# Low parts of the full-width weight tiles formed by an accumulating transfer

## The chip, the cores and the metric

The kernel runs on one core of one Trainium2 chip. The metric is device time in microseconds (us): the median of several executions. A core has five engines that run side by side and wait for each other only where data passes between them: TensorE (PE, matrix products; PEld is its weight load), VectorE (DVE), ScalarE (ACT), GpSimd (POOL) and SyncE (SP, which issues most transfers). A transfer (DMA) moves data between the chip's memory and the on-chip SBUF, or inside SBUF.

## The reference, cut to what matters

One decoder layer over 1024 prompt tokens and 8 single-token sequences, 1032 columns in all, model width 1024, everything in float32:

```python
h = rms_norm(x, ln1); proj = h @ w_in             # q, k, v, xr, xg, g_att, g_lru
o_att = window_attention(q, k, v, ...) @ w_o_attn
o_lru = (rg_lru(causal_conv(xr)) * gelu(xg)) @ w_o_lru
x = x + (sigmoid(g_att) * o_att + sigmoid(g_lru) * o_lru) @ w_out
x = x + (silu(h2 @ w_gate) * (h2 @ w_up)) @ w_down
x = x + sigmoid(rms_norm(x, ln3) @ w_ple_gate) * (p @ w_ple)
```

The outputs are the new activations, the last window of keys and values, the recurrent state and the last rows before the convolution.

## The kernel before, in words

TensorE multiplies in a reduced float format (fp32r). To keep float32 accuracy every operand is split in a high part, rounded to that format, and a low part, the raw value minus the high part. A product is then three passes: high by high, high by low, low by high (`passes`, L334). One full product (`product`, L343) is 8 row blocks x 3 passes x 3 column thirds of 344, that is 72 matmuls; the third pass of its first row block is the first that reads the low part of the weights.

Weight tiles follow a written list, `plan` (L155): 4 q tiles, 16 gate tiles, 16 xr/xg tiles, 8 `oa` tiles, 8 `ol`, 8 `out`, the gate/up pairs of the feed-forward part (which have a splitting of their own, L244 to L269), 32 `down` tiles, 2 `pp` and 8 `pg`. The q, gate, xr/xg, ol, out, pp and pg tiles are 1024 wide, 62 in number; `oa` (512) and `down` (768 or 640) are narrower. `weights` (L327) is called as a product is written down: it loads the raw tile two places ahead in the list (`wload`, L198) and starts `wsplit` (L223) of the next tile. Raw, high and low tiles have three buffers each (tags wraw, whi, wlo). `split` (L180) forms the high part on POOL (L181) and the low part on DVE (L187); two ticks lie between them, and L187 is queued behind the last eviction of a product (`issue_after(st["mul"])`). The first tile of the list is formed in the startup with `ordered=True` (L183).

The text of the kernel gives each instruction its engine and a place in an order of generators (`at`, `spawn`, `tick`); from this the Tile framework's planner makes each engine's queue with costs and ready times of its own, and may move an instruction forward when it holds it to be ready. Edges by `keep` and `issue_after` bind it. On the chip each engine works through its queue strictly in order, and an instruction that waits holds up everything behind it.

Besides weight tiles, ACT takes results out of PSUM, forms high parts of activations (L357) and does all exponentials, tanh and the like; POOL multiplies the attention weights (L728) and parts of the recurrence, and issues the transfers that double the q and k rows (`halves`, L632, the issue in L638). Those 20 transfers are the only ones issued by POOL.

Of the kernel before, what the change touches and what calls it, by code (L numbers as in the profile page):

```python
# [13 lines left out]
AF = mybir.ActivationFunctionType  # L14
ALU = mybir.AluOpType
# [35 lines left out]
def body(ctx, tc, d):  # L51
    nc = tc.nc
    V, A, G, TE, DMA = nc.vector, nc.scalar, nc.gpsimd, nc.tensor, nc.sync.dma_start
# [38 lines left out]
    def f(t):  # L92
        return t.bitcast(F32)
# [86 lines left out]
    def split(raw, hi, lo, a, b, ordered=False):  # L180
        G.tensor_scalar(hi[:, a:b], raw[:, a:b], 1.0, 0.0, ALU.mult, ALU.add)  # L181
        if ordered:
            keep(V.tensor_tensor(lo[:, a:b], raw[:, a:b], f(hi[:, a:b]), ALU.subtract))  # L183
            return
        yield 2
        with tc.issue_after(st["mul"]):
            V.tensor_tensor(lo[:, a:b], raw[:, a:b], f(hi[:, a:b]), ALU.subtract)  # L187
# [35 lines left out]
    def wsplit(i, ordered=False):  # L223
        if i >= len(plan):
            return
        if paired(i):
            yield from pair_pre(i)
            return
        n = src(plan[i])[1]
        raw = raws.pop(i)  # L230
        hi, lo = whl(str(i))
        ready[i] = (hi, lo)
        yield from split(raw, hi, lo, 0, n, ordered)
# [676 lines left out]
    def recur(c, ps):  # L910
# [17 lines left out]
        wh = wp.tile([P, 256], F32R, tag="axh", name=f"axh{c}", bufs=1)  # L928
        wl = wp.tile([P, 256], F32R, tag="axl", name=f"axl{c}", bufs=1)
        yield from split(wr, wh, wl, 0, 256)  # L930
        xch = hi_of(f"xc{c}", xc)
        yield REC[3]
# [477 lines left out]
```

## Time and profile before

| | |
|---|---|
| time, median of 3 runs (lowest, highest) | 1600.42 us (1599.16, 1601.59) |
| the profiled execution's own time | 1602.14 us |
| its span, first to last instruction | 1600.4 us |
| TensorE busy | 1573.8 us (98%) |
| VectorE, ScalarE, GpSimd busy | 899.9, 527.9, 412.4 us |
| granted TensorE clock, mean | 0.995 |

Busy is the time in which an engine executes; an engine that stands at 98% leaves 26.6 us of the span without a matmul. In the lists of groups each line gives the busy total, the mean of one instruction in ns, and the idle time of that engine just before such instructions with what ended it. In a timeline the columns are start, duration, engine, line, operation, tile written and tiles read, shape, and in brackets the idle time before.

### The profile page before, as it was taken

Reading aid. Unit: us, or ns where it says so; the run is one execution under the profiler, and the core shown is the slowest. Engines: PE = TensorE matmul, PEld = TensorE weight load, DVE = VectorE, ACT = ScalarE, POOL = GpSimd, SP = SyncE. Lnnn points to the kernel's source line nnn. Section 1 sums busy time; section 2 is a strip of 40 time slices with the busy share of each in tenths; the row PEclk is TensorE's granted clock in tenths of the full one; section 3 lists DMA queues with packets and bytes.
Section 4 is the critical chain, followed back from the end, with each engine's and each line's share of the span. In section 5 each row is a group of like instructions: output and inputs, shape, how many; then the busy total and the mean of one; then the engine's idle time right before and its main releaser. Section 6 shows DMA issues by size and latency. Waiting matters only on the chain.

```text
span 1600.4 us, 25144 instructions
## 1 busy us (share of the span) xinstructions
PE 1573.8 (98%) x10763; PEld 1549.6 (97%) x10763; DVE 899.9 (56%) x1047; ACT 527.9 (33%) x785; POOL 412.4 (26%) x291
## 2 busy tenths in 40 slices
PE   8999999999999999999989999999998999999998
PEld 7999999999999999999989999999998999999998
DVE  8668555645778684355765555555555432436534
ACT  5652332314646651132633333333333110103201
POOL 4342211212232231012144444444442110011100
PEclk9899999999999999999999999999999999999999
DMA  5364122221111342333122222222225421312121
GB/s 191 79 166 125 54 103 83 83 73 35 55 43 34 109 159 81 106 123 129 53 80 80 80 80 80 80 80 79 78 75 215 167 93 57 116 55 88 30 90 53
DMA packets 46733, 145.78 MB, mean 91 GB/s; under 512 B 6645, under 2 KB 11038, under 8 KB 46622
## 3 DMA queue, kind: packets, MB, share of 16 engines
q1 hardware_dynamic: 44786, 138.80, 25.7%
q0 software_dynamic: 1600, 5.29, 1.6%
q8 instruction: 84, 1.38, 0.3%
q14 instruction: 27, 0.22, 0.0%
q10 hardware_dynamic: 236, 0.10, 0.0%
HBM read 107.45 MB, written 31.44 MB: 87 GB/s over the span
## 4 chain that ended last, share of the span: by engine, by line
PE 90%; DVE 3%; issue 2%; ACT 2%; DMA 1%; POOL 1%; SPq 0%; DVEq 0%; POOLq 0%; ACTq 0%
PE psd L338 15%; PE psgt L338 10%; PE psol L338 6%; PE psout L338 6%; PE psxr L338 6%; PE pspg L338 5%; PE psxg L338 5%; PE psq L338 2%; PE pspp L338 1%; PE o L751 1%; PE psrx L943 1%; PE psoa L1018 1%; PE pt L736 1%; PE psu10x L320 1%; PE psg6x L320 1%
## 5 line engine op out<-in xcount | busy, mean ns | idle before, releaser
L181 POOL TENSOR_SCALAR wh<-wr 128x1024 fp32r<-128x1024 f32 (+3 forms) x102 | 104.8, 1028 | 629.5 <-PE psd L338 222.8
L187 DVE TENSOR_TENSOR wl<-wr,wh 128x1024 fp32r<-128x1024 f32 (+3 forms) x101 | 118.8, 1178 | 10.9 <-POOL wh L181 10.9
L1075 DVE TENSOR_TENSOR x<-psd,x 128x1032 f32<-128x1032 f32 x32 | 39.4, 1232 | 128.8 <-PE psd L338 128.8
L1204 POOL TENSOR_TENSOR g<-g,n2r 128x1032 f32<-128x1032 f32 x22 | 54.2, 2466 | 142.5 <-DVE wl L242 126.1
L249 POOL TENSOR_TENSOR wsA<-wr 128x512 f32<-128x512 f32 x22 | 38.6, 1756 | 131.9 <-DVE wl L242 126.6
L253 DVE TENSOR_TENSOR wl<-wr,wh 128x1024 fp32r<-128x1024 f32 x22 | 26.9, 1225 | 67.3 <-ACT wh L250 67.3
L722 ACT ACTIVATE s<-s,st 128x256 f32<-128x256 f32 (+1 forms) x64 | 31.1, 489 | 77.8 <-DVE st L717 76.5
L728 POOL TENSOR_TENSOR s<-s,st 128x1024 f32<-128x1024 f32 (+1 forms) x16 | 28.6, 1787 | 98.1 <-DVE st L727 87.9
L240 ACT ACTIVATE wh<-wsA 128x1024 fp32r<-128x1024 f32 x22 | 23.3, 1060 | 91.5 <-issue 80.7
L242 DVE TENSOR_TENSOR wl<-wsB,wh 128x1024 fp32r<-128x1024 f32 x22 | 39.7, 1805 | 4.5 <-ACT wh L240 4.5
L252 POOL TENSOR_TENSOR wsA<-wsA,wr 128x512 f32<-128x512 f32 x22 | 38.7, 1757 | 1.6
L250 ACT ACTIVATE wh<-wr 128x1024 fp32r<-128x1024 f32 x22 | 23.3, 1060 | 47.2 <-PE psout L338 5.7
L1294 ACT ACTIVATE pg<-pg 128x1032 f32<-128x1032 f32 (+3 forms) x10 | 9.0, 895 | 88.3 <-DVE pg L96 79.9
L1217 DVE TENSOR_TENSOR u<-u,g 128x516 f32<-128x516 f32 x33 | 34.9, 1058 | 3.8 <-POOL g L1204 2.4
L96 DVE TENSOR_TENSOR pg<-pspg,n3r 128x1032 f32<-128x1032 f32 x7 | 8.6, 1232 | 48.9 <-PE pspg L338 48.9
L262 POOL TENSOR_TENSOR wsB<-wr,wr 128x512 f32<-128x512 f32 x22 | 33.8, 1538 | 7.9 <-DVE wl L242 7.9
L96 DVE TENSOR_TENSOR xr<-psxr,r1r 128x1032 f32<-128x1032 f32 x8 | 9.9, 1233 | 44.9 <-PE psxr L338 44.9
L1043 DVE SCALAR_TENSOR_TENSOR gl<-gl,psol 128x1032 f32<-128x1032 f32 x8 | 9.8, 1229 | 43.3 <-PE psol L338 43.3
L263 POOL TENSOR_TENSOR wsB<-wr,wsA 128x512 f32<-128x512 f32 x22 | 34.1, 1551 | 0.1
L925 DVE SCALAR_TENSOR_TENSOR xc<-xr,sm,xc 128x1021 f32<-128x1021 f32 (+2 forms) x24 | 30.7, 1277 | 5.9 <-ACT xc L919 5.9
L709 DVE TENSOR_TENSOR s<-s,bias 128x512 f32<-128x512 f32 (+1 forms) x32 | 19.7, 653 | 24.1 <-PE s L705 23.8
L970 POOL TENSOR_TENSOR hg<-h,xg 128x1032 f32<-128x1032 f32 x8 | 25.5, 3186 | 26.3 <-DVE h L966 22.7
(1691 smaller groups left out, 5065.1 us busy)
## 6 DMA issues: line engine op xcount, KB each, us to landing
wr<-w_in SPq DMA_DIRECT2D x36, 512.0 KB, 3.6
ad<-u SPq DMA_DIRECT2D x22, 516.0 KB, 2.6
a<-ad SPq DMA_DIRECT2D x22, 516.0 KB, 5.3
wr<-w_gate SPq DMA_DIRECT2D x22, 512.0 KB, 3.6
wr<-w_up SPq DMA_DIRECT2D x22, 512.0 KB, 3.6
sg<-gt SPq DMA_DIRECT2D x16, 516.0 KB, 2.8
gl<-sg SPq DMA_DIRECT2D x16, 516.0 KB, 4.5
wr<-w_down SPq DMA_DIRECT2D x16, 384.0 KB, 3.1
```

The lines of the kernel that those rows point to most:

```text
L181: G.tensor_scalar(hi[:, a:b], raw[:, a:b], 1.0, 0.0, ALU.mult, ALU.add)
L187: V.tensor_tensor(lo[:, a:b], raw[:, a:b], f(hi[:, a:b]), ALU.subtract)
L242: V.tensor_tensor(hl[1][:, :n], raw, f(hl[0][:, :n]), ALU.subtract)
L249: G.tensor_tensor(s[:, n:2 * n], b[:, :n], b[:, n:2 * n], ALU.add)
L252: G.tensor_tensor(s[:, :n], s[:, n:2 * n], a[:, :n], ALU.subtract)
L262: G.tensor_tensor(s[:, :n], a[:, :n], b[:, :n], ALU.subtract)
L263: G.tensor_tensor(s[:, n:2 * n], a[:, n:2 * n], e["s21"][:, :n], ALU.subtract)
L320: TE.matmul(ps[:, c, :QC], ww[:, w], xx[:, c * QC:(c + 1) * QC], start=first and kk == 0 and n == 0, stop=True if not last else kk == nk - ...
L338: TE.matmul(ps[:, c, :CH], ww[:, w], xx[:, c * CH:(c + 1) * CH], start=first and n == 0, stop=last and n == 2)
L1075: V.tensor_tensor(v3(t), ps[:, :, :CH], v3(t), ALU.add)
L1204: G.tensor_tensor(t, t, r, ALU.mult)
L1217: V.tensor_tensor(o, o, g, ALU.mult)
```

## The change

In `split`, a full-width tile (b == 1024) that is not the ordered one no longer has its low part formed by DVE. ACT writes minus the high part into the low tile, and a transfer issued from POOL's queue adds the raw tile onto it in SBUF. The two ticks and the edge behind the last eviction are gone for these tiles, 61 in number. The ordered tile and the narrower tiles stay as they were.

```diff
         G.tensor_scalar(hi[:, a:b], raw[:, a:b], 1.0, 0.0, ALU.mult, ALU.add)
         if ordered:
             keep(V.tensor_tensor(lo[:, a:b], raw[:, a:b], f(hi[:, a:b]), ALU.subtract))
+            return
+        if b == 1024:
+            A.activation(lo[:, a:b], f(hi[:, a:b]), AF.Copy, scale=-1.0)
+            G.dma_start(f(lo[:, a:b]), raw[:, a:b], accum_op=ALU.add)
             return
         yield 2
         with tc.issue_after(st["mul"]):
```

## Rows read from the trace of the kernel before

**Rows 1.** The page, part 1: busy us of each engine, share, instructions

```profile
PE 1573.8 (98%) x10763; PEld 1549.6 (97%) x10763; DVE 899.9 (56%) x1047; ACT 527.9 (33%) x785; POOL 412.4 (26%) x291
```

**Rows 2.** What PE waited for: total us, times, longest

```profile
PE r1ps L384 <- ACT r1sh L357: 2.7, 1, 2.7
...
PE r1ps L385 <- DVE r1sl L365: 1.7, 1, 1.7
...
PE psoa L1018 <- DVE wl L187: 0.4, 1, 0.4
```

**Rows 3.** Groups by form: busy us, mean ns, idle before and releasers

```profile
L187 DVE TENSOR_TENSOR wl<-wr,wh 128x1024 fp32r<-128x1024 f32 x61 | 82.8, 1358 | 6.4 <-POOL wh L181 6.4
L181 POOL TENSOR_SCALAR wh<-wr 128x1024 fp32r<-128x1024 f32 x62 | 72.6, 1171 | 383.7 <-PE psol L338 81.5 <-PE pspg L338 51.5 <-PE psxr L338 43.6
...
L250 ACT ACTIVATE wh<-wr 128x1024 fp32r<-128x1024 f32 x22 | 23.3, 1060 | 47.2 <-PE psout L338 5.7 <-PE psu2y L320 2.1 <-PE psu5y L320 2.1
```

**Rows 4.** Timeline of the startup, DVE, ACT and PE

```profile
36.81 2.35 DVE L187 TENSOR_TENSOR wl<-wr,wh 128x1024 fp32r<-128x1024 f32 x2
39.08 1.22 DVE L365 TENSOR_TENSOR r1sl<-x,r1sh 128x1032 fp32r<-128x1032 f32 x1
...
36.93 1.06 ACT L357 ACTIVATE r1sh<-x 128x1032 fp32r<-128x1032 f32 x1 [6.20 <-DVE x L569]
...
40.36 0.65 PE L385 MATMUL r1ps<-r1sl,ones_r 128*128 128x344 f32 x1 [1.66 <-DVE r1sl L365]
```

**Rows 5.** Timeline in the ol stage, POOL, SP's queue and PE

```profile
624.90 1.05 POOL L181 TENSOR_SCALAR wh<-wr 128x1024 fp32r<-128x1024 f32 x1 [10.30 <-PE psol L338]
...
627.72 0.33 SPq L212 DMA_DIRECT2D wr<-w_out  x1
...
647.60 1.05 POOL L181 TENSOR_SCALAR wh<-wr 128x1024 fp32r<-128x1024 f32 x1 [10.30 <-PE psol L338]
...
648.76 0.48 PE L338 MATMUL psol<-hg0h,wl 128*128 128x344 f32 x2
```

**Rows 6.** Timeline around the first ol product, POOL, ACT and PE

```profile
579.60 1.04 POOL L181 TENSOR_SCALAR wh<-wr 128x1024 fp32r<-128x1024 f32 x1 [4.60 <-DMA wr<-w_ol]
...
580.71 1.05 ACT L357 ACTIVATE hg3h<-hg 128x1032 fp32r<-128x1032 f32 x1
...
592.04 0.63 PE L338 MATMUL psol<-hg0h,wl 128*128 128x344 f32 x3
```

**Rows 7.** POOL's own transfers, L638: ns min/median/max of the issue; landing in us

```profile
L638 POOL DMA_DIRECT2D kd<-kh x4: 522/533/725, 70.6 to 72.4; - x4
...
DMA to landing us min/median/max: 2.9/4.4/7.7
```

**Rows 8.** Transfers issued by SP: count, KB each, median us to landing

```profile
wr<-w_in SPq DMA_DIRECT2D x36, 512.0 KB, 3.6
...
wr<-w_oa SPq DMA_DIRECT2D x8, 256.0 KB, 2.7
```

**Rows 9.** Stage 135 to 341 us: busy us (instructions) of PE, PEld, DVE, ACT, POOL

```profile
135.00:341.00 206.00, 205.33 (x1285) 193.08 (x1284) 115.49 (x251) 61.32 (x202) 41.29 (x30) 1.00 0.23 79
```

**Rows 10.** Timeline of one attention unit, DVE, POOL and PE

```profile
161.25 1.29 DVE L742 TENSOR_TENSOR p<-pt,p 128x512 fp32r<-128x512 f32 x2 [1.58 <-ACT p L738]
...
163.35 1.90 POOL L728 TENSOR_TENSOR s<-s,st 128x1024 f32<-128x1024 f32 x1 [10.20 <-DVE st L727]
...
163.62 0.39 PE L751 MATMUL o<-p,vth 128*128 128x512 f32 x1
...
172.62 1.03 PE L736 MATMUL pt<-ident,s 128*128 128x128 f32 x8
```

**Rows 11.** Startup windows: busy us as in rows 9, then granted clock, DMA share, GB/s

```profile
35.00:41.00 6.00, 1.66 (x6) 1.01 (x5) 5.20 (x5) 1.98 (x2) 0.00 (x0) 0.75 0.31 79
41.00:45.00 4.00, 4.00 (x17) 4.00 (x16) 0.00 (x0) 2.94 (x7) 0.01 (x1) 0.52 0.36 143
...
55.00:59.00 4.00, 4.00 (x18) 3.93 (x17) 2.12 (x3) 2.53 (x4) 1.36 (x1) 0.57 0.43 131
```

## The prediction

> **What bounds the kernel now.** I read the page's first part, then what PE waited for, then the timelines around the weight tiles. PE is busy 1573.8 us of a span of 1600.4 us [rows 1], so 26.6 us are all that a better hidden splitting could give back, and PE's list of waits says how little of that belongs to the low parts [rows 2]: the only PE wait that names a low part of weights is 0.4 us, at a narrow tile that the change leaves alone. One more is indirect. At 36.81 us DVE forms two low parts in 2.35 us, and the low part of the first norm's sum (r1sl) starts behind them at 39.08, though its input r1sh was ready at 37.99 (36.93 + 1.06) [rows 4]; PE waits 1.66 us for r1sl. The reader is to see in the rest that weights are formed far ahead. POOL writes a high part at 624.90, the moment a product ends and gives its buffer back; two products later the same happens at 647.60 (11.35 us each), and only in the product that starts then is the tile of 624.90 read, in its low part at 648.76 [rows 5]: 23.9 us of lead.
>
> **The change part by part.** The sum is made against the profiled execution, 1602.14 us (span 1600.4 and 1.74 around it); the median shown is 1600.42, 1.72 below, and I carry the difference over to it.
>
> *Removed from DVE:* 61 subtractions, 82.8 us in all, 1.36 us each [rows 3]. DVE is busy 899.9 us, off the bound, so 59 of them are worth nothing to PE. The two at 36.81 are worth the delay of r1sl: 39.08 - 37.99 = 1.09 us. What is late next is r1sh itself, which PE already waits for (2.7 us), and it does not depend on them. The gain is at least nothing (if the planner puts other DVE work in the place) and at most 1.66 us, the whole wait. I take -1.1.
>
> *Added on ACT:* 61 copies with factor -1, same shape and kind as the copy of 1.06 us [rows 3]: 65 us on an engine busy 527.9. They wait for POOL's high part (1.17 us on average), and behind them in ACT's queue stand the evictions and exponentials. In the startup the cover is ACT's idle gap of 6.20 us before r1sh [rows 4]. In the attention stage, where 13 tiles are formed, ACT is busy 61.3 of 206 us, 30% [rows 9]; if the moments are unrelated, 4 of 13 copies meet work and push it back by up to 1.06 us. The shortest cover there is between DVE's low part of the probabilities, done at 162.54, and the matmul that uses them at 163.62: 1.08 us [rows 10]. 1.06 fits in 1.08, barely. Below nothing is excluded, since ACT only gets more work. I take 0; without cover it is 4 x 1.06 = 4.2 us, and it is the second rival that says when.
>
> *Added on POOL:* 61 issues. The trace has 20, of half as many partitions, at 0.52 to 0.73 us [rows 7]. Twice the rows, and a second read for the addition, give at most 4 x 0.52 = 2.1 us; I take 1.0, twice the short one. Before it POOL waits for ACT's copy, 1.06 us when ACT is free. Behind it stand other high parts, which have the lead above, and in the attention stage the multiplication L728: it ends at 165.25 and PE transposes its result at 172.62 [rows 10], 7.4 us of cover against about 2. Cost 0.
>
> *The transfer itself* does not occur in the trace. Nearest rows: POOL's own SBUF transfers of 258 KB land in 2.9 to 7.7 us, median 4.4 [rows 7]; loads of 512 KB take 3.6 and of 256 KB 2.7 [rows 8], so 256 KB more cost 0.9. From 4.4: +0.9 for 512 KB, +1.8 for reading the destination as well, 7.1 us. Lower end 2.9; upper end, all doubled twice, 4 x 7.7 = 30.8. From the start of the high part the low part is then ready after 1.05 + 1.06 + 1.0 + 7.1 = 10.2 us, against a lead of 23.9 in the ol stage. The shortest lead of a full-width tile is at the first ol product, which follows the half-length oa products: high part at 579.60, first use at 592.04 [rows 6], 12.4 us. 2.2 us are left there, and ACT stands in a close row of copies (580.71 is one of them) that can eat them: 0, at most a few us, see the first rival. The raw buffer comes free when the transfer has landed instead of when DVE is done (SP's next load went out at 627.72, 2.8 us after the high part began [rows 5]); 7.4 us later costs nothing while a buffer is needed again only three products, 34 us, after. The DMA engines are busy 23% in the attention stage [rows 9]; a load that shares them with the new transfer lands later by at most its 7.1 us, inside the same 34.
>
> The DMA page of the Trainium skill (DMA: Bandwidth & Descriptors, section Anatomy of one DMA — SWDGE (gpsimd) path) gives such transfers about 2.0 us plus bytes over 436 GB/s, an estimate of 3.2 us for 512 KB. The 258 KB would be 2.6 us by it, where this trace has a median of 4.4, so I go by the trace; by the page's figure the sum is the same and the tight tile has 6 us to spare.
>
> *Narrow tiles, the feed-forward pairs and the ordered tile:* unchanged, 0.
>
> *Sum:* -1.1 + 0 + 0 + 0 = -1.1 us: 1601.0 for an execution like the profiled one, 1599.3 for the median.
>
> **The rivals.**
>
> *The transfer is late (slower).* Everything but the landing takes 3.1 us, so the tight tile waits from a landing of 9.3 us on. For: the longest landing of the small ones is 7.7 us, and the second read is unknown. At twice 7.7, 15.4 us, that product starts 15.4 + 3.1 - 12.4 = 6.1 us late, and the time is 1599.3 + 6.1 = 1605.4. From 20.8 us on every ol product waits too; at 30.8 the three-product loop of 34 us grows by 10, 3.3 us a product, 200 us over 61 tiles, about 1800. Against that end: the longest landing in the trace is a quarter of it.
>
> The SBUF page of the skill (SBUF — State Buffer, section Who interferes with whom) says that GpSimd writes the descriptors of such a transfer and is shut out while VectorE runs a two-port instruction. It would add the length of that instruction to a landing. Here the issues beside busy DVE took 0.73 us at most, against 0.52 [rows 7], so I give it no chance of its own.
>
> *The queue heads (slower; the rival on the other side).* Place: ACT's queue in the attention stage. The planner may put the copy ahead of work that is ready while POOL is not: then ACT stands for the high part (1.17 us [rows 3]) and the copy (1.06), 2.23 against the 1.08 of cover [rows 10], 1.15 us of PE each time. It decides when more than 4 of the 13 tiles do it. For: the edge that kept the low part behind the evictions is gone, and ACT has no pin for the copy. Against: ACT is idle 70% of that stage [rows 9], and PE waits for no line of it now [rows 2]. 4 tiles: +4.6, 1603.9; all 13: +15, 1614; I take 7, +8.1, 1607.
>
> *The clock (faster).* After PE's idle stretch the granted clock is 0.75 and then 0.52 for 4 us, the lower of its two levels (1.2 of 2.4 GHz), and again 0.57 at 55 to 59 [rows 11]. A gap that is 1.1 us shorter may not bring it down: 4 x 0.48 = 1.9 us, 3.0 in all, 1597.4; with the second dip (4 x 0.43 = 1.7) 4.7, 1595.7. Against: the wait of 2.7 us for r1sh stays, and so most of the gap.
>
> That the change does not do what it says is no rival: the condition can only be met by those 61 tiles.
>
> **How the numbers follow.** About 0.2%, 3.2 us, is what a measurement of this kernel can tell from no change. Forecast 0.56 (its own range 1597 to 1602: 0.47 within 0.2%, 0.05 below, 0.04 above); queue heads 0.18 (0.15 slower, 0.03 within); late transfer 0.11 (0.09 slower, 0.02 within); clock 0.12 (0.10 faster, 0.02 within); another order of the planner, either way, 0.03 (0.02 faster, 0.01 slower). Faster 0.17, same 0.54, slower 0.29. The range reaches down past the clock's 1595.7 to 1594, and up past 1607 to 1611; it leaves out the end of the late transfer and the case of all 13 tiles.
>
> **What would show it.** Right: DVE's full-width group L187 gone; r1sl at about 38.0 in the startup; landing of the new transfers 5 to 9 us; no PE wait that names wl of more than 1 us; PE's busy time as before. The late transfer: a PE wait on the transfer of the low part at the first psol product. Queue heads: ACT's copies with idle time before them that ends with POOL's wh, and PE waits in L751 or L736. The clock: windows 41 to 45 and 55 to 59 near 1.0. The prediction is wrong if PE's waits outside the first 60 us grow by more than 3 us.

## The result and the profile after

The changed kernel takes 1613.49 us (median of 4 runs, 1612.45 to 1614.40) against 1601.01 for the kernel before, run beside it: a ratio of 1.0080 [1.0067, 1.0092], about 12.5 us slower. The prediction was 1599.3, with a range of 1594 to 1611. The profiled execution took 1612.45 us, its span 1610.7, so 10.3 us are to be found between the two traces (executions of one kernel lie up to 3 us apart). From here on line numbers are those of the changed kernel, 4 higher after L183.

The page of after, part 1, answers [rows 1]:

```profile
PE 1578.0 (98%) x10763; PEld 1552.8 (96%) x10763; DVE 822.4 (51%) x986; ACT 588.7 (37%) x846; POOL 464.7 (29%) x352
```

The work moved as forecast: DVE lost 77.5 us, ACT gained 60.8. PE is busy for 4.2 us more with the same number of matmuls, so some of them ran at a lower clock. The rest is in its waits (total, times, longest), to be read beside [rows 2]:

```profile
PE s L707 <- DVE dsb L794: 5.8, 1, 5.8
PE psgt L342 <- issue: 3.0, 1, 3.0
PE vt L617 <- ACT wl L186: 2.9, 1, 2.9
...
PE r1ps L388 <- ACT r1sh L361: 1.0, 1, 1.0
PE s L707 <- DVE oA0l L767: 0.9, 1, 0.9
```

Two waits are new, the first two, and neither names a weight tile. The third, in the startup, does name ACT's copy, but it stands for the 2.4 us that PE waited there for DVE's vraw before: here vraw ends at 51.80 us and the copy at 51.82. The start of each stage's first matmul says where they count:

```
us from the span's start    before    after    after - before
gates and attention          92.8      91.9     -0.9
xr/xg                       341.2     352.4    +11.2
oa                          542.4     553.5    +11.1
gate/up pairs               772.4     783.5    +11.1
down                       1225.5    1237.4    +11.9
pp                         1480.9    1490.5     +9.6
end of the last matmul     1595.7    1606.0    +10.3
```

The gate and attention stage alone loses 12.1 us; all that follows it together gains 0.9.

**The first wait, at 105 us.** The timeline of ACT and POOL in after (start, duration; in brackets the idle time before and who ended it):

```profile
102.62 0.47 ACT L498 ACTIVATE sbias<-bias 128x384 f32<-128x384 f32 x1
...
104.92 1.24 POOL L181 TENSOR_SCALAR wh<-wr 128x1024 fp32r<-128x1024 f32 x1 [6.59 <-PE psgt L342]
...
106.19 1.06 ACT L186 ACTIVATE wl<-wh 128x1024 fp32r<-128x1024 f32 x1 [3.10 <-POOL wh L181]
107.16 1.01 ACT L680 ACTIVATE q3raw<-psq 128x1032 f32<-128x1032 f32 x1
```

and that of PE:

```profile
104.65 0.63 PE L342 MATMUL psgt<-x7h,wl 128*128 128x344 f32 x3
108.27 0.72 PE L342 MATMUL psgt<-x0h,wh 128*128 128x344 f32 x3 [2.98 <-issue]
```

The planner put the copy of tile 7 (the fourth gate tile) ahead of q3raw, the eviction of the last q product. The copy waits for POOL's high part, that for a free high buffer, and the buffer comes free only when PE ends its product at 104.9. So the eviction stands behind work that waits for PE, and PE's next product waits for the accumulator that the eviction empties. (The profile names no releaser for this wait; PE starts 0.1 us after the eviction ends, at 108.17.) In the kernel before, ACT evicts at once:

```profile
103.58 0.47 ACT L494 ACTIVATE sbias<-bias 128x384 f32<-128x384 f32 x1
103.95 1.02 ACT L676 ACTIVATE q3raw<-psq 128x1032 f32<-128x1032 f32 x1
```

**The second wait, at 250 us.** DVE in after:

```profile
254.42 1.23 DVE L96 TENSOR_TENSOR gt<-psgt,r1r 128x1032 f32<-128x1032 f32 x1 [6.06 <-DMA sg<-gt]
255.57 0.27 DVE L794 TENSOR_TENSOR dsb<-ds,sbias 64x128 f32<-64x128 f32 x1
```

An eviction of a gate product needs a row buffer, and the row comes free when an earlier gate tile has been stored (sg<-gt). Behind it in DVE's queue stands dsb, which empties the accumulator that PE wants for the next scores. Before, the same instruction came without a wait:

```profile
246.59 1.23 DVE L96 TENSOR_TENSOR gt<-psgt,r1r 128x1032 f32<-128x1032 f32 x1
```

SP's queue in after (the decode step's cache loads KT and VS, its stores o_ks and o_vs, the gate's store):

```profile
223.60 0.34 SPq L216 DMA_DIRECT2D wr<-w_in  x1
224.06 0.67 SPq L197 DMA_DIRECT2D KT<-kc  x1
224.83 0.44 SPq L197 DMA_DIRECT2D VS<-vc  x1
225.32 13.11 SPq L775 DMA_DIRECT2D VS<-vdr  x1
238.54 0.37 SPq L777 DMA_DIRECT2D o_ks<-KT  x1
239.00 0.66 SPq L842 DMA_DIRECT2D sg<-gt  x1
251.87 0.34 SPq L778 DMA_DIRECT2D o_vs<-VS  x1
```

and before:

```profile
217.56 0.33 SPq L212 DMA_DIRECT2D wr<-w_in  x1
218.01 0.67 SPq L193 DMA_DIRECT2D KT<-kc  x1
219.27 0.26 SPq L193 DMA_DIRECT2D VS<-vc  x1
219.59 2.96 SPq L771 DMA_DIRECT2D VS<-vdr  x1
227.09 2.43 SPq L773 DMA_DIRECT2D o_ks<-KT  x1
230.39 0.38 SPq L838 DMA_DIRECT2D sg<-gt  x1
242.87 0.34 SPq L774 DMA_DIRECT2D o_vs<-VS  x1
```

The landings of the 16 stores sg<-gt, that is the time that the profile gives from issue to arrival, in before and in after:

```profile
DMA to landing us min/median/max: 2.6/2.8/15.0
DMA to landing us min/median/max: 2.6/2.6/15.3
```

The longest in each is the store here: from 230.39 to 245.4 in the kernel before, 1.2 us ahead of its need at 246.59, and from 239.0 to 254.3 in after. What is in its way is the load VS<-vc of 127 rows. In a stretch of before in which little else is on the way, the window's last columns (granted clock, DMA share, GB/s) are:

```profile
236.00:240.00 4.00, 4.00 (x29) 3.98 (x28) 2.56 (x8) 1.61 (x6) 0.00 (x0) 1.00 0.06 27
```

A share of 0.06 is one of 16 DMA engines. The page DMA: Bandwidth & Descriptors of the Trainium skill (section Why a DMA increments its semaphore by 16 and not by 1) says that a transfer uses the largest number of engines up to 16 that divides the slowest dimension of both its sides; 127 is prime, so one, and the 0.06 agrees. From its issue to that of o_vs, which waits for it and for the single row VS<-vdr behind it, 23.6 us pass in before and 27.0 in after. In after SP also stands 13.1 us in the issue of VS<-vdr (3.0 before), so the store is issued 8.6 us later. That isn't what decides: the store lands 2.5 us after the issue of o_vs in before and 2.4 in after, and 2.4 to 2.6 after it in the six other kernels below that keep the load whole and whose traces list this store's landing, where it was issued 12 to 16 us ahead of o_vs. It lands when the load is through.

**The clock after it** (windows; granted clock is the third number from the end):

```profile
250.00:256.00 6.00, 0.23 (x3) 0.10 (x1) 1.54 (x3) 0.00 (x0) 0.88 (x1) 0.78 0.79 186
256.00:262.00 6.00, 6.00 (x20) 5.10 (x21) 3.89 (x13) 1.19 (x5) 0.00 (x0) 0.50 0.78 269
262.00:270.00 8.00, 8.00 (x46) 7.38 (x46) 1.63 (x4) 3.17 (x11) 1.90 (x1) 0.90 0.01 2
```

When PE resumes after 5.8 us of standing, 6 us run at 0.50, the lower level (1.2 of 2.4 GHz), and the next 8 at 0.90: 3.0 + 0.8 = 3.8 us. The sum for the stage: 2.98 - 0.65 at 105 us (there was a gap of 0.65 at 111 before), 5.8 at 250, 0.7 more in small gaps at 135 and 143 us, and 3.8 of clock give 12.6 against 12.1.

### The profile page after: what moved, and what is told of

The parts are those of the page before. It is cut to its first block, busy times and chain, and to the rows that moved or that the text cites. A ratio compares the mean times of both kernels' runs of the same rounds, so it can differ in the third digit from the quotient of the medians.

```text
span 1610.7 us, 25263 instructions
## 1 busy us (share of the span) xinstructions
PE 1578.0 (98%) x10763; PEld 1552.8 (96%) x10763; DVE 822.4 (51%) x986; ACT 588.7 (37%) x846; POOL 464.7 (29%) x352
## 3 DMA queue, kind: packets, MB, share of 16 engines
q0 software_dynamic: 10384, 37.27, 12.1%
## 5 line engine op out<-in xcount | busy, mean ns | idle before, releaser
L186 ACT ACTIVATE wl<-wh 128x1024 fp32r<-128x1024 f32 x61 | 64.5, 1059 | 226.5 <-POOL wh L181 226.4
L187 POOL DMA_DIRECT2D wl<-wr x61 | 54.1, 892 | 89.7 <-ACT wl L186 74.2
L191 DVE TENSOR_TENSOR wl<-wr,wh 128x768 fp32r<-128x768 f32 (+2 forms) x40 | 36.0, 903 | 4.5 <-POOL wh L181 4.5
```

The lines of the kernel that those rows point to most:

```text
L186: A.activation(lo[:, a:b], f(hi[:, a:b]), AF.Copy, scale=-1.0)
L187: G.dma_start(f(lo[:, a:b]), raw[:, a:b], accum_op=ALU.add)
```

## The experiments

Theory after the traces: the loss has two places, ACT's queue at 105 us (the copy) and SP's at 250 us. The rivals for the second: SP's order, which the planner changed; the transfers themselves, by landing late or by sharing the DMA engines; the cache load. All ratios are against the kernel before on the same chip.

**1. Only the first 20 tiles; only the last 42.**

```diff
-        if b == 1024:
+        if b == 1024 and i < 20:        # the other kernel: i >= 20
```

> Only the 19 tiles of q, gate and attention (plan index below 20) take the low part by copy and transfer; the other 42 are formed by DVE as before. Theory (the loss is made in the gate and attention stage alone): 1612 to 1615, PE idle about 3 us near 105 us and about 6 us near 250 us as in the changed kernel. Rival (the loss needs all 61 tiles, by load on the DMA engines or by the clock over the whole span): 1600 to 1606.

> Only the 42 tiles from plan index 20 on (recurrent inputs, ol, out, pp, pg) take the new path; q, gate and attention tiles as before. Theory: 1598.5 to 1601.5, no PE wait over 1 us that names a weight tile after 341 us. Rival (all 61 share the loss): 1606 to 1610.

Measured: 1612.18, 1.0073 [1.0058, 1.0088], gaps of 2.98 us at 105 and 5.48 at 251; and 1601.96, 1.0010 [1.0000, 1.0020], 0.5 us above the range of its theory. The 19 tiles of the q and gate products make the loss; the other 42 cost 0.1%, 0.2% at most.

**2. The two halves of the change apart.** First DVE forms minus the high part and the transfer stays; then ACT copies as in the change and DVE adds.

```diff
-            A.activation(lo[:, a:b], f(hi[:, a:b]), AF.Copy, scale=-1.0)
+            yield 2
+            with tc.issue_after(st["mul"]):
+                V.tensor_scalar(lo[:, a:b], f(hi[:, a:b]), -1.0, None, ALU.mult)
```
```diff
-            G.dma_start(f(lo[:, a:b]), raw[:, a:b], accum_op=ALU.add)
+            yield 2
+            with tc.issue_after(st["mul"]):
+                V.tensor_tensor(lo[:, a:b], raw[:, a:b], f(lo[:, a:b]), ALU.add)
```

> All 61 tiles; minus the high part is formed by DVE, behind the evictions as the subtraction was, instead of by ACT, and the transfer adds the raw tile as in the change. SyncE's order in the gate stage is then that of the kernel before. Theory (one half of the loss is ACT's queue head near 105 us, the other half a spill store that SyncE issues late because its order changed): both gone, 1599 to 1603. Rival (the transfer itself, its DMA load or its late release of the raw buffer): the wait near 250 us and most of the loss stay, 1607 to 1613.

> All 61 tiles; ACT copies minus the high part as in the change, and DVE adds the raw tile, behind the evictions, instead of the transfer. SyncE's order in the gate stage is that of the kernel before. Theory: if ACT stands with the copy ahead of the last q eviction near 105 us also here, PE idles 3 us there and 1603 to 1606 comes out; the wait near 250 us is gone. Rival (ACT alone makes the whole loss): 1610 to 1614. Second rival (ACT costs nothing, all is the transfer): 1598 to 1601.

Measured: 1616.31, 1.0102 [1.0086, 1.0119]; and 1605.71, 1.0031 [1.0020, 1.0042]. PE's waits in the first:

```profile
PE s L709 <- DVE dsb L796: 6.0, 1, 6.0
...
PE psgt L344 <- DMA wl<-wr: 2.6, 1, 2.6
```

and ACT's timeline in the second, the same queue head as in the change, with 3.6 us of PE behind it and nothing at 250 us:

```profile
104.39 0.47 ACT L500 ACTIVATE sbias<-bias 128x384 f32<-128x384 f32 x1
107.96 1.06 ACT L186 ACTIVATE wl<-wh 128x1024 fp32r<-128x1024 f32 x1 [3.09 <-POOL wh L181]
108.92 1.01 ACT L682 ACTIVATE q3raw<-psq 128x1032 f32<-128x1032 f32 x1
```

So the first wait belongs to ACT's copy. Behind this gap of 3.6 us the granted clock reads 0.75 (109 to 112 us) and 0.68 (112 to 115), where after the 2.98 us of the change it stays at 1.00; which goes some way to explain that this kernel is 5.5 us slower than the one before. My theory of the second, SP's changed order, falls: with SP's order around the cache loads as it was before, the transfer alone brings the wait of 6.0 us. It also brings others, since the low part starts later there; why q3sh comes 2.3 us late in that kernel was not followed up.

**3. The copies behind the evictions.**

```diff
+            with tc.issue_after(st["ev"]):   # the last eviction of a q product
                 A.activation(lo[:, a:b], f(hi[:, a:b]), AF.Copy, scale=-1.0)
```

> The change, with each of ACT's copies put into ACT's queue behind the last eviction of a q product. Theory (ACT's queue head at 105 us, 3.0 us of PE and the clock after it): q3raw is evicted without a wait, the gap of 3.0 us at 105 us is gone and that at 49 us too; the wait of about 6 us near 250 us stays. 1607 to 1611. Rival (the moment of the copy doesn't matter, POOL's high part is what is late): 1612 to 1615, with the gap still there.

Measured: 1627.31, 1.0169 [1.0153, 1.0184]. Both expectations missed:

```profile
PE psgt L343 <- DMA wl<-wr: 8.7, 2, 6.1
PE s L708 <- DVE dsb L795: 5.3, 1, 5.3
PE psq L343 <- DMA wl<-wr: 3.3, 1, 3.3
```

The gap at 105 us went, but now three low parts are late. One of them: the copy comes right after the eviction of q1 (71.9), POOL issues the transfer only at 77.3, behind an addition of 3.3 us, and PE, which wants the tile from 79.1 on, gets it at 82.4. Among the q tiles there is no room between the eviction and the low part's use.

**4. The load of 127 rows cut: in the changed kernel, in that of experiment 3, and in the kernel before.**

```diff
-        load(VS[0:127], d["vc"])
+        load(VS[0:112], d["vc"][0:112])
+        load(VS[112:127], d["vc"][112:127])
```

> The change, with the load of the 127 rows of the value cache cut into 112 and 15 rows. In both kernels the 127 rows trickle at a DMA share of 0.06, one of 16 engines, for some 20 us, and the spill store behind them lands after 15 us. Theory (the transfer frees the raw buffer late, so SyncE starts this load 6 us later, and the store that frees a row is behind it on that one engine): the store lands in under 8 us, DVE's wait of 6.1 us for it and PE's gap of 5.8 us near 250 us go, 1604 to 1607. Rival (the late load of weights itself, or the share of the DMA engines that the 61 transfers take): the gap near 250 us stays over 3 us, 1609 to 1614.

> The change with both edits: copies behind the evictions, and the value cache load cut in 112 and 15 rows. Theory (the two waits are the whole loss): 1597.5 to 1601.5, the startup's gain of 0.9 us at most left over. Rival (a third cost, DMA load or the clock, holds part of the loss): 1603 to 1608.

> Control: the kernel before with only the value cache load cut in 112 and 15 rows. Theory: no PE wait there to remove (the store lands 1.2 us before its row is needed), 1599 to 1602. Rival (the cut load is worth something by itself): below 1598.5.

Measured: 1603.88, 1.0019 [1.0010, 1.0028]; 1617.64, 1.0109 [1.0094, 1.0123], outside both its ranges; control 1600.82, 1.0002 [0.9993, 1.0011]. SP's queue in the first (the change with the load cut):

```profile
224.84 0.67 SPq L197 DMA_DIRECT2D KT<-kc  x1
225.60 1.07 SPq L197 DMA_DIRECT2D VS<-vc  x2
226.73 0.23 SPq L776 DMA_DIRECT2D VS<-vdr  x1
230.65 0.37 SPq L778 DMA_DIRECT2D o_ks<-KT  x1
233.00 0.34 SPq L843 DMA_DIRECT2D sg<-gt  x1
```

and DVE's eviction:

```profile
249.20 1.23 DVE L96 TENSOR_TENSOR gt<-psgt,r1r 128x1032 f32<-128x1032 f32 x1
```

The loads leave as late as in after (224.84), and yet the eviction does not wait; none of its 16 gate stores takes more than 7.9 us to land. Of the 12.5 us over the kernel before 3.1 are left (1603.88 against 1600.81 on the same chip), so 9.4 come back: the wait of 5.8 and the 3.8 of clock behind it make 9.6. In the kernel before, the same cut is worth nothing, since the store was there in time, by 1.2 us. The kernel of experiment 3 gains 9.7 from the cut as well, and its three late low parts stay.

**5. The cache loads earlier, uncut.**

```diff
-    at(ATT_D + int(8.5 * ATT_I), att_decode())
+    at(ATT_D + int(7.5 * ATT_I), att_decode())
```

> The change, with the decode chain put 20 ticks earlier (7.5 instead of 8.5 steps), so that its cache loads stand in SyncE's queue ahead of the weight load that waits for a transfer; the 127-row load is whole. Theory (the loss near 250 us is made of this load being late, not of its shape alone): loads at about 208 us instead of 224, DVE's wait of 6.1 us gone or under 1 us, 1603 to 1606. Rival (wherever it stands, the 127-row load holds up a store by 15 us and the wait only moves): 1608 to 1613.

Measured: 1611.38, 1.0066 [1.0051, 1.0082]: the rival. VS<-vc was issued at 215.98, 3.3 us earlier than in the kernel before, and still the store behind it took 18.5 us, and another instruction of DVE waited for the row:

```profile
247.55 1.29 DVE L713 TENSOR_TENSOR s<-s,bias 128x512 f32<-128x512 f32 x2 [6.76 <-DMA sg<-gt]
```

So the late start is not needed for a loss here; whether it would do alone was not tried. From the issue of VS<-vc to that of o_vs pass 23.6, 23.7, 23.7 and 23.8 us in the kernels without new transfers there (before, the last 42 tiles alone, tiles 1 and 2 alone, and the ACT copy with DVE's addition) and 26.6 to 28.9 in the five uncut ones with them. That fits transfers that put their part on the one engine that is already the slow one; no row here shows the load engine by engine.

**6. What is left: tile 7 back to DVE, with the load cut; and tiles 1 and 2 alone.**

```diff
-        if b == 1024:
+        if b == 1024 and i != 7:        # the other kernel, load uncut: i in (1, 2)
```

> The change with the value cache load cut in 112 and 15 rows, and with tile 7 alone (the second gate-tile after q3, whose copy stands in ACT's queue ahead of q3's eviction) formed by DVE as before. Theory (that one queue head is what is left of the loss, 1603.9 against 1600.8): the gap of 3.0 us at 105 us shrinks below 1 us, 1600 to 1602. Rival (another copy takes its place, or the rest lies elsewhere): 1603 to 1605.

> The kernel before with only tiles 1 and 2 (the second and third q tile) on the new path: the part from which the prediction had its gain of 1.1 us. Theory: r1sl starts at 38 us, PE's waits in the first 60 us fall by about 1 us, 1598.5 to 1600.5. Rival (other startup waits take it back): 1600.3 to 1602.

(Tile 7 is the fourth gate tile; the wording of the expectation is wrong there.) Measured: 1600.12, 0.9997 [0.9989, 1.0006]; and 1598.81, 0.9993 [0.9984, 1.0002]. With one tile out of ACT's way q3raw is evicted at once and the gap is gone:

```profile
102.64 0.47 ACT L498 ACTIVATE sbias<-bias 128x384 f32<-128x384 f32 x1
103.00 1.02 ACT L680 ACTIVATE q3raw<-psq 128x1032 f32<-128x1032 f32 x1
```

One copy of 61 costs about 3 us: against the kernel before on the same chip the time goes from 3.1 us above (1603.88, 1600.81) to 0.1 below (1600.12, 1600.25), 3.2 us, of which 2.3 are PE's gap at 105 us (2.98 to 0.66). With the two causes taken away the change is even with the kernel before. The two startup tiles alone give what the prediction saw there: r1sl at 38.04, PE's wait for it 0.85 instead of 1.66, the gate stage 0.9 us earlier. The median is 1.4 us below the kernel before, but the interval holds 1, so a version that beats both kernels is not shown.

## Why the prediction was wrong

**The step that failed** is the one on the raw buffer, in "The transfer itself": "7.4 us later costs nothing while a buffer is needed again only three products, 34 us, after", and "a load that shares them with the new transfer lands later by at most its 7.1 us, inside the same 34". Both sentences ask only who waits for the buffer and for the load. The buffer did come free later, 7.9 us after the start of the high part (215.70 to 223.60) instead of 3.7 (213.90 to 217.56), and no weight tile was late by it. The high parts, in after and in before:

```profile
215.70 1.06 POOL L181 TENSOR_SCALAR wh<-wr 128x1024 fp32r<-128x1024 f32 x1 [8.28 <-issue]
213.90 1.05 POOL L181 TENSOR_SCALAR wh<-wr 128x1024 fp32r<-128x1024 f32 x1 [9.17 <-issue]
```

But the load that waits for the buffer holds SP's queue, and the transfers share DMA engines with other loads: the cache load started 5.6 us later and ran 3.4 longer, and the store landed 8.9 later (254.3 against 245.4). Its need came 1.8 us later too (248.36 against 246.59, the stage being late by the first wait and smaller ones), and its margin was 1.2 us: 8.9 - 1.8 - 1.2 = 5.9, against the 6.06 that DVE waited. How much the late start and the sharing would each cost alone is not shown. The prediction looked at the mean DMA share of the stage, 0.23 [rows 9], where one engine of 16 was busy for 20 us on end; and it read only the weight loads' landings [rows 8], not the store of 15.0 us among 16 of 2.8. This step is 9.4 of the 12.5 us, by the run with the load cut; the next one is 3.2, and what is left of both is -0.1.

**"Added on ACT: I take 0"** failed too, by about 3.2 us as the runs with and without tile 7 have it. The rival named this mechanism, ACT's queue ahead of ready work, but put it in the attention stage with waits in L751 or L736; it came before that stage, at 105 us, at a product's first matmul. Size and count were wrong as well: 1.15 us a time in more than 4 of 13 tiles, where it was one tile at 3.0 us. POOL's high part itself waited for PE's buffer. So the high part (1.24 us), the copy (1.06) and the eviction (1.01) came one after another behind the end of the running product, with nothing to cover them. The rival's 1607 was nearer than the forecast by accident: most of the loss has the other cause.

**The startup term** was about right: -0.9 at the start of the gate stage against -1.1, with PE's wait for r1sl down from 1.7 to 0.8. Other waits of the startup moved too (r1sh from 2.7 to 1.0), so one pair of traces would be weak evidence. But the gate stage starts at 92.6 to 93.6 us in the three kernels whose tiles 1 and 2 are formed as before (before, the last 42, the control), and at 91.3 to 92.4 in the six that form them by copy and transfer without other late tiles. In the medians a gain of this size isn't resolved.

**The transfer's own price** was smaller than taken: issue 0.88 us (1.0 taken), landing 4.5/4.6/10.9 us minimum, median, maximum (7.1 taken). No PE wait names the low part of a full-width weight tile after 341 us, so the tight place at the first ol product was none, and the rival of the late transfer fell there. The estimate of 3.2 us by the page DMA: Bandwidth & Descriptors of the Trainium skill (section Anatomy of one DMA — SWDGE (gpsimd) path) is below the shortest landing, 4.5.

**The clock** was told only as a possible gain. In the startup the windows of [rows 11] do read 1.00, 1.00 and 0.96 in after, but the dip had moved: 51 to 55 us reads 0.62, and 1.00 before. What came of it is within the -0.9. In the attention stage, behind PE's stall, the clock took 3.8 us.

**A row misread.** The wait of 0.4 us is not the only one on PE's list that names a low part of weights: psk waits 1.1 us for wlo, a startup tile split by code of its own (L439). The change leaves it alone, so the sum is not touched.

## What to carry to other kernels

A step that frees a buffer later can be paid by everything that stands behind the waiting instruction in its queue, not only by the buffer's next reader: list what follows in that queue, and which of it has least margin. Before adding transfers, look for the longest landing of each group, not its median, and for stretches at a share of one engine; the load of 127 rows was such a stretch, and cut in 112 and 15 rows it held nothing up. Before putting a copy into the queue of an engine that empties accumulators, ask what its input waits for: tile 7's waited for the end of the running product, and the eviction that the next product needed stood behind it.

## What the runs showed of the hardware

An SBUF to SBUF transfer that adds 512 KB landed 4.6 us after its issue, 4.5 at the least; the median weight load of the same size in the same trace takes 3.5 to 3.8, by tensor. Behind a PE stall of 5.8 us the granted clock was 0.50 and then 0.90, 3.8 us more; behind one of 3.6 us it read 0.75 and 0.68 for 6 us, and behind one of 2.98 us 1.00. A load of 127 rows of 4 KB stood on one DMA engine for 20 us and more; as 112 and 15 rows it landed in 6.2 and 5.7. A store of 516 KB issued while it ran landed only after it, in 15.0 to 18.5 us where the median of its kind is 2.6 to 3.0.
